# A Strassen-tiled pooling trunk: the second phase's operands stored and loaded, an inner product added in its last block, weight sums and short copies moved

## The chip, the cores and the metric

One core of a Trainium2 chip runs the whole kernel in one launch. The metric is device microseconds of that core, lower is better. The engines are called by the profile's names: PE is the matrix engine (TensorE; PEld its weight loads), DVE VectorE, ACT ScalarE, POOL GpSimd, SP the engine that issues most DMAs.

## The reference, cut to what matters

With DEPTH = 1 only the pooling mixer runs, then a final RMS norm. x is (1, 4096, 1024) in float32.

```python
normed = rms_norm(x, norm_w)
u, gate = split(normed @ pool_in_w, 2)                     # 1024 -> 2 x 1024
pooled = [trailing_mean(u[:, g], 2 << g) for g in 0..3] - u   # windows 2, 4, 8, 16; 256 channels each
mixed = einsum('bsgc,gcd->bsgd', pooled, group_w) + group_b
h = x + (mixed * pool_scale * silu(gate)) @ pool_out_w
out = rms_norm(h, final_norm_w)
```

The group map is folded into the input weights at the start of the kernel, since averaging over time commutes with a map over channels.

## The kernel before, in words

**Three phases.** Steps are written (kind, block, product). In the phases "a" and "b" the rows of x stand in four blocks of 1024; "a" makes the products of the first half of the output channels, "b" those of the second half, from the same normalised x with other weights. Phase "o" is the output projection over eight blocks of 512 rows, followed by the residual, the final norm and the stores. A block's matrix product is one level of Strassen-Winograd: seven products P1 to P7 of half-size operands in the order P1, P2, P7, P6, P5, P4, P3 (`ORDER_IN`). The left operands (weights' sums) are kept in `w`, the right ones (x's sums) are made for each block: "11", "12", "21", "22" are quarters of normalised x; P7's operand replaces "21", P6's (S2) is called "2", P5's (S1) replaces "11", P3's (S4, `form_s4`) replaces "12".

**Splitting.** Each operand is a sum of two reduced-precision float32r parts, so a product is three passes. `split` writes the high part with a ScalarE copy and the low part with a VectorE subtraction; both read the full operand of 128x1024 twice per product (h = 0, 1). A plain product is 48 matmuls of 128x512 (`mm3`, line 807). An inner product (`product_seven`, line 753) applies Strassen once more inside P7: 84 matmuls of 128x256, whose operands `split_seven` makes with sums of half tiles and two further splits, and whose partial sums ScalarE moves between banks. In phase "b" this is done in blocks 1 and 2. Its weight sums take three of the eleven `st` buffers (`kept_in`) and a part of P7's weight buffer, which `load_plain` and `split_plain` fill again with the plain weight for block 3.

**Storage.** Quarters P1, P2, P7 and P4 of normalised x are written to DRAM (`sd`) from GpSimd's queue while phase "a" splits them, and phase "b" reads them back (`load_saved`) on SP's queue; there S2, S1 and S4 are formed on VectorE again. All temporaries come from two pools of equal tiles, eleven `st` and eight `vt`: `take` hands out the tile that was given back longest ago, and a DMA into it waits until its last user is done. Loads are issued three steps ahead (`load_reach`), splits one step ahead (`split_reach`).

**Work beside the products.** Pooling (`pool`) runs on VectorE a step or more after its half block is evicted; a ScalarE copy of 128x32 takes the previous half block's last 16 rows from `tails`, another writes the new ones. `save_t3` forms a weight sum for phase "b" (loads of two stored sums, one subtraction, a store) after step (a, 2, P7). `make_wo` forms the output weights' sums in blocks 1 and 2 of phase "b" and stores them (`wod`); `load_w` reads and splits each into `w[i]` after the last block has used that buffer. The order of instructions on each engine is fixed when the program is built, by the program's order, dependences and hints (`tc.issue_after`: not ahead of that instruction on its engine).

**The end.** From the third output block on, `steady` writes out the order by hand. In the last block the results are normalised in pieces, and the inner part of P2 adds its results with `add_inner` from a spare bank, which TensorE uses again for the next inner product.

Of the kernel before, what the change touches and what calls it, by code (L numbers as in the profile page):

```python
# [10 lines left out]
F32 = mybir.dt.float32  # L11
# [75 lines left out]
def kernel(  # L87
# [115 lines left out]
    def split(dst, src):  # L203
# [17 lines left out]
        for i in range(P1, P7 + 1)  # L221
# [3 lines left out]
            i: [dram.tile([P, 2, H], F32, name=f"sd{b}_{i}_{h}") for h in range(2)]  # L225
            for i in (P1, P2, P7, P4)
        }
# [96 lines left out]

    def save_t3():

        for h in range(2):
# [246 lines left out]
    def load_saved(b, i):  # L574
# [5 lines left out]
        return us  # L580

    def load_in(q, b, i):
        s = xs[b]
        if i == P1:
            s["11"] = load_saved(b, P1) if q else load_x(b, 0, 0)
        elif i == P2:
            s["12"] = load_saved(b, P2) if q else load_x(b, 0, 1)
        elif i == P7:
            s["21"] = load_saved(b, P7) if q else load_x(b, 1, 0)
        elif i == P6:  # L590
            s["22"] = load_saved(b, P4) if q else load_x(b, 1, 1)

    def form_in(q, b, i):

        s = xs[b]
        if i in (P1, P2):
            if q == 0:
                for u in s["11" if i == P1 else "12"]:
                    normalize(b, 0, u)
        elif i == P7:  # L600
            if q == 0:
                for h in range(2):
                    normalize(b, 1, s["21"][h])
                    sub(s["21"][h], s["11"][h], s["21"][h])
        elif i == P6:
            s["2"] = [take(pool=early if (q, b) == (0, 0) else None) for _ in range(2)]
            for h in range(2):
                if q == 0:
                    normalize(b, 1, s["22"][h])
                sub(s["2"][h], s["22"][h], s["21"][h])  # L610
            if not inner_in(q, b, P7):
                for u in s.pop("21"):
                    give(u)
            if q == 0:
                give(rstd.pop(b))
        elif i == P5:
            for h in range(2):
                add(s["11"][h], s["2"][h], s["11"][h])
            if (q, b) != (0, 0) and not inner_in(q, b, P7):
                for u in s.pop("2"):  # L620
                    give(u)

    def inner_in(q, b, i):

        return q == 1 and 0 < b < NB - 1 and i == P7

    def split_in(q, b, i):
        s = xs[b]
        if inner_in(q, b, i):
            return split_seven(s)  # L630
        key = {P1: "11", P2: "12", P6: "2", P7: "21", P5: "11", P4: "22", P3: "12"}[i]
# [62 lines left out]
    def form_seven(stage):  # L694
# [31 lines left out]
        if stage == 3:  # L726
            for u in seven.pop("raw"):
                give(u)

    def load_plain():  # L730
        seven["plain"] = take("p (n k c) -> p n k c", n=2, k=2)
        sync.dma_start(out=seven["plain"][:, 0], in_=t3d[0][:, :, 0:256])

    def split_plain():
        u = seven.pop("plain")
        home = [w[P7][0][:, v, :, 0:256] for v in range(2)]
        copy(home[0], u[:, 0])
        sub(home[1], u[:, 0], home[0].bitcast(F32))
        give(u)

# [319 lines left out]
    def pool(b, q, half, vs, sgs):  # L1060
# [4 lines left out]
        for g in range(2):  # L1065
# [301 lines left out]
    def evict_o(b, i, sets):  # L1367
# [13 lines left out]
        for j in range(2):  # L1381
# [24 lines left out]
            if last:  # L1406
                factors.append(late_factor(half, j, parts))
                if i == P4 and j == 1 or i == P3 and j == 0:
# [65 lines left out]
    def run(n, between=None, behind=None, seeds=4):  # L1474
# [7 lines left out]
        else:  # L1482
            q = 0 if kind == "a" else 1
            if inner_in(q, b, i):
# [6 lines left out]
                product_seven(split_up.pop(n), sets["v"], next_half, next_half)  # L1491
                if b == NB - 2:
                    give_kept(*places_in)
# [8 lines left out]
            if inner_in(q, b, i):  # L1502
                form_s4(b)
                for u in xs[b].pop("2"):
                    give(u)
# [3 lines left out]
    def steady(n):  # L1509
# [87 lines left out]
        elif i == P2:  # L1597
# [4 lines left out]
            ready[P4] = next_op("p (s a b) -> p s a b", **whole)  # L1602
            split(ready[P4], s["22"])
            give(s.pop("22"))
            if final:
                norm_row(b - 1, 0, 1)
            InOrder.on = not final
            product_out(P2, ready.pop(P2), sets, False)
            evict_o(b, P2, sets)
        elif i == P5:  # L1610
            sub(s["12"], s["12"], s["11"])
# [6 lines left out]
        elif i == P4:  # L1618
            if not final:
                ahead["12"] = load_y(c, 0, 1)  # L1620
# [233 lines left out]
    def split_reach(kind, b, i):  # L1854
        if kind == "b" and 0 < b < NB - 1 and i == P6:
            return 0
        return 2 if kind == "o" and (b, i) != (0, P1) else 1

    def row_plan(b):
# [16 lines left out]
        (1, P6): lambda: sum_inner(P7),  # L1876
        (1, P5): lambda: split_weight(P7, P7, P6),
        (1, P4): lambda: (split_weight(P7, P5, P3), keep_temps(P7)),
    }
    forming_seven = (P7, P6, P5, P4)  # L1880

    for n in range(2, len(steps)):
# [72 lines left out]
        if kind in ("a", "b"):  # L1955
# [3 lines left out]
            if kind == "b" and b == NB - 1:  # L1959
                load_w(wod, i)  # L1960
            if kind == "b" and b in (1, 2) and i == P7:
                load_wo(b - 1)
                if b == NB - 2:
                    load_plain()
# [3 lines left out]
            if kind == "b" and b == NB - 2 and i == P4:  # L1968
                with tc.issue_after(latest_copy[0]), tc.issue_after(latest_split[0]):
                    split_plain()  # L1970
            if kind == "b" and b == NB - 1 and i == P3:
# [57 lines left out]
```

## Time and profile before

| what | before |
|---|---|
| time, median of three runs | 907.2 us (907.1 to 908.36) |
| the profiled execution's own time | 907.23 us |
| its span | 905.4 us |
| granted TensorE clock | 0.998 |
| PE / DVE / ACT / POOL busy | 895.8 / 757.0 / 517.5 / 118.5 us |
| DMA | 180.49 MB, mean 199 GB/s |
| first matmul of phase "a", of "o", last matmul's end | 32.6, 613.0, 898.4 us |

The span is what the instructions cover; the execution's own time adds what lies around it. Busy time is summed over instructions; an engine's idle time matters only where TensorE waits for it. Buffer numbers are left out, so `st` stands for eleven buffers. L79 is a helper through which VectorE, ScalarE, GpSimd and SP record everything, so their groups are told apart by tiles.

### The profile page before, as it was taken

The numbers are of one execution on the slowest core, as the hardware profiler recorded it, in microseconds if no ns is written. First come the engines' busy times: TensorE is split into PE (matmuls) and PEld (weight loads), VectorE is DVE, ScalarE is ACT, GpSimd is POOL, SyncE is SP. The second block draws the span as 40 slices with busy tenths as digits, with TensorE's granted clock in tenths as the row PEclk, the third lists the DMA queues.
The fourth block names the chain that finished last, engine by engine and source line by source line (L and its number), as shares of the span: only waits on it lengthen the run. The fifth ranks groups of instructions, "written<-read, shape, count | busy, mean of one in ns | idle before, by whom it ended". The sixth has DMA issues, their size and how long they took to land.

```text
span 905.4 us, 12216 instructions
## 1 busy us (share of the span) xinstructions
PE 895.8 (99%) x4518; PEld 791.1 (87%) x4518; DVE 757.0 (84%) x925; ACT 517.5 (57%) x853; POOL 118.5 (13%) x208
## 2 busy tenths in 40 slices
PE   9999999999999999999999999999999999999996
PEld 7888888888888888889889888888889899999995
DVE  3899995985995999797599499599798878888797
ACT  7869547547445565346545636654657466565464
POOL 0020100100110000000000000001133333343330
PEclk9999999999999999999999999999999999999999
DMA  9987767577675453333554474638483865945953
GB/s 343 401 305 226 273 239 241 187 274 233 235 267 198 164 199 103 99 112 111 202 199 135 179 279 143 197 117 239 143 236 88 212 180 147 233 153 131 259 181 116
DMA packets 71692, 180.49 MB, mean 199 GB/s; under 512 B 6608, under 2 KB 24656, under 8 KB 71632
## 3 DMA queue, kind: packets, MB, share of 16 engines
q1 hardware_dynamic: 54976, 132.50, 42.6%
q0 software_dynamic: 15936, 46.16, 17.6%
q10 hardware_dynamic: 720, 1.06, 0.3%
q8 instruction: 35, 0.57, 0.3%
q14 instruction: 25, 0.20, 0.1%
HBM read 118.86 MB, written 60.83 MB: 198 GB/s over the span
## 4 chain that ended last, share of the span: by engine, by line
PE 87%; DVE 5%; ACT 3%; DMA 2%; issue 2%; POOL 0%; SPq 0%; DVEq 0%; ACTq 0%; POOLq 0%
PE bank L807 78%; PE bank L949 5%; DVE vt L79 2%; PE bank L753 2%; DVE op L79 2%; DMA st<-yd 1%; PE bank L447 1%; DVE st L79 1%; ACT op L79 1%; DMA early<-in_wut 1%; ACT st L79 1%; ACT w L79 0%; ACT vt L79 0%; DMA st<-wod 0%; DVE w L79 0%
## 5 line engine op out<-in xcount | busy, mean ns | idle before, releaser
L807 PE MATMUL bank<-op,w 128*128 128x512 f32 x2592 | 560.9, 379 | 0.1
L807 PEld LDWEIGHTS bank<-op,w 128*128 128x128 f32 x2592 | 489.4, 189 | 70.3 <-ACT vt L79 0.5
L807 PE MATMUL bank<-w,op 128*128 128x512 f32 (+1 forms) x1044 | 230.5, 377 | 0.0
L807 PEld LDWEIGHTS bank<-w,op 128*128 128x128 f32 x1044 | 192.3, 189 | 25.0
L79 DVE TENSOR_TENSOR op<-st,op 128x1024 fp32r<-128x1024 f32 x116 | 141.0, 1222 | 49.7 <-ACT op L79 49.3
L79 ACT ACTIVATE op<-st 128x1024 fp32r<-128x1024 f32 x116 | 121.4, 1051 | 68.7 <-PE bank L807 27.6
L79 ACT ACTIVATE op<-vt 128x1024 fp32r<-128x1024 f32 x67 | 70.4, 1053 | 59.3 <-DVE vt L79 38.7
L79 ACT ACTIVATE vt<-bank 128x512 f32<-128x512 f32 (+1 forms) x124 | 69.6, 580 | 48.0 <-PE bank L807 44.2
L79 DVE TENSOR_TENSOR op<-vt,op 128x1024 fp32r<-128x1024 f32 x67 | 80.9, 1221 | 17.5 <-ACT op L79 17.4
L79 DVE TENSOR_TENSOR st<-st,st 128x1024 f32<-128x1024 f32 (+1 forms) x55 | 63.9, 1181 | 17.6 <-ACT st L79 16.8
L79 POOL DMA_DIRECT2D vt<-in_x x26 | 23.3, 937 | 390.7 <-DVE vt L79 353.8
L79 ACT ACTIVATE bank<-bank 128x512 f32<-128x512 f32 (+1 forms) x78 | 38.7, 498 | 43.5 <-PE bank L807 32.1
L79 DVE TENSOR_TENSOR vt<-bank,vt 128x512 f32<-128x512 f32 (+1 forms) x94 | 54.2, 603 | 7.1 <-PE bank L949 4.6
L79 ACT ACTIVATE st<-bank 128x512 f32<-128x512 f32 (+1 forms) x58 | 33.0, 587 | 31.2 <-PE bank L807 17.4
L79 ACT ACTIVATE st<-st 128x1024 f32<-128x1024 f32 x33 | 34.8, 1056 | 22.6 <-DVE st L79 19.6
L79 DVE TENSOR_TENSOR st<-bank,st 128x512 f32<-128x512 f32 (+1 forms) x68 | 41.2, 625 | 7.4 <-PE bank L807 4.1
L79 DVE TENSOR_TENSOR st<-st,vt 128x1024 f32<-128x1024 f32 (+1 forms) x36 | 41.6, 1175 | 2.2 <-DMA vt<-rd 2.2
L949 PEld LDWEIGHTS bank<-w,op 128*128 128x128 f32 x312 | 40.4, 191 | 1.7
L949 PE MATMUL bank<-w,op 128*128 128x256 f32 x312 | 41.1, 275 | 0.0
L79 DVE TENSOR_TENSOR w<-st,w 128x1024 fp32r<-128x1024 f32 (+1 forms) x27 | 31.6, 1182 | 9.3 <-ACT w L79 9.2
L79 DVE TENSOR_TENSOR_SCAN vt<-vt,window 128x1040 f32<-128x1040 f32 x16 | 38.0, 2381 | 0.3 <-DMA yd<-vt 0.3
L79 DVE TENSOR_TENSOR vt<-vt 128x1024 f32<-128x1024 f32 (+3 forms) x42 | 37.6, 898 | 0.1
(115 smaller groups left out, 720.7 us busy)
## 6 DMA issues: line engine op xcount, KB each, us to landing
st<-in_xt SPq DMA_DIRECT2D x28, 512.0 KB, 6.2
sd<-st POOLq DMA_DIRECT2D x28, 512.0 KB, 4.4
st<-sd SPq DMA_DIRECT2D x26, 512.0 KB, 4.5
st<-in_x SPq DMA_DIRECT2D x21, 512.0 KB, 6.3
yd<-st SPq DMA_DIRECT2D x19, 512.0 KB, 2.9
vt<-yd SPq DMA_DIRECT2D x17, 512.0 KB, 10.4
out<-vt POOLq DMA_DIRECT2D x17, 512.0 KB, 3.3
st<-wod SPq DMA_DIRECT2D x16, 512.0 KB, 4.3
```

The source lines that it names most:

```text
L79: r = f(*args, **kwargs)
L447: latest[0] = nc.tensor.matmul(ps, a[:, kk, 2 * j + t, :], maps, start=t + m == 0, stop=t == 1 and m == len(pairs) - 1,).ins
L753: latest[0] = nc.tensor.matmul(cell(n, c).rearrange("p (a s) -> p a s", s=2), x1, x2, start=i == P1 and k + m == 0, stop=k == 1 and m == 2 ...
L807: latest[0] = nc.tensor.matmul(ps, a, b, start=start and n == 0, stop=stop and n == 2, skip_group_check=True).ins
L949: latest[0] = nc.tensor.matmul(ps, x1, x2, start=start and k + n == 0, stop=k == 1 and n == 2, skip_group_check=True,).ins
```

## The change

It has these parts. (1) Phase "a" stores the operands of all seven products, except block 0's S2, and phase "b" loads them instead of forming them; block 0's S2 is still formed there from "22" and "21". An operand's tiles are given back after its split. (2) The inner P7 is used in block 3 as well, so the plain weight is no longer restored and the three `st` buffers are held until block 3's P7. (3) In block 3 of phase "b" the output weights are loaded and split in other groups: P1's after P7, P2's and P7's after P6, P6's and P5's after P5; their splits come behind the step's evictions. (4) The weight sum T3 is formed in two halves, after (a, 1, P3) and (a, 2, P3). (5) In phase "b" the short copy from `tails` runs on GpSimd. (6) In the output phase, the first inner addition of the last block precedes P2's evictions, P4's split comes after them, one row normalisation moves to P4's stage, and two of the inner weight splits move one step later.

```diff
-            for i in (P1, P2, P7, P4)
+            for i in range(P1, P7 + 1)
+            if (b, i) != (0, P6)
...
 def load_w(src, i):
-            split(w[i][h], u)
+            with tc.issue_after(evicted[0]):
+                split(w[i][h], u)
...
+    operand = {P1: "11", P2: "12", P7: "21", P6: "2", P5: "11", P4: "22", P3: "12"}
     def load_in(q, b, i):
         s = xs[b]
-        if i == P1:
-            s["11"] = load_saved(b, P1) if q else load_x(b, 0, 0)
...
-        elif i == P6:
-            s["22"] = load_saved(b, P4) if q else load_x(b, 1, 1)
+        if q and (b or i not in (P6, P4)):
+            s[operand[i]] = load_saved(b, i)
+        elif q:
+            if i == P6:
+                s["22"] = load_saved(b, P4)
...
     def inner_in(q, b, i):
-        return q == 1 and 0 < b < NB - 1 and i == P7
+        return q == 1 and b > 0 and i == P7
...
 def split_in(q, b, i):
-        if i == P6 and (q or b):
+        if i == P6 and q == 0 and b:
             form_s4(b)
-        if i not in (P1, P2, P7, P6):
+        if q and (b or i != P7) or i not in (P1, P2, P7, P6):
             for u in s.pop(key):
                 give(u)
...
 def pool(b, q, half, vs, sgs):
+            elif q:
+                gpsimd.tensor_copy(out=v[:, :, 0:HIST], in_=tails[:, g])
             else:
                 copy(v[:, :, 0:HIST], tails[:, g])
...
 def evict_o(b, i, sets):
         if inner and i == P2:
             inner["rows"] = [hs[b][0, j][:, 0] for j in range(2)]
+            if final:
+                add_inner(0, (0, 0))
...
-        if inner and i == P2:
+        if inner and i == P2 and not final:
             add_inner(0, (0, 0))
...
 def form(n):
-        if kind in ("a", "b"):
-            form_in(kind == "b", b, i)
+        if kind == "a":
+            form_in(b, i)
+        elif (kind, b, i) == ("b", 0, P6):
+            s["2"] = [take() for _ in range(2)]
+            for h in range(2):
+                sub(s["2"][h], s["22"][h], s["21"][h])
...
 def steady(n), i == P2:
-            split(ready[P4], s["22"])
-            give(s.pop("22"))
-            if final:
-                norm_row(b - 1, 0, 1)
+            if not final:
+                split(ready[P4], s["22"])
+                give(s.pop("22"))
             InOrder.on = not final
             product_out(P2, ready.pop(P2), sets, False)
             evict_o(b, P2, sets)
+            if final:
+                split(ready[P4], s["22"])
+                give(s.pop("22"))
...
 i == P4:
+            if final:
+                norm_row(b - 1, 0, 1)
...
 forming = {
-        (1, P5): lambda: split_weight(P7, P7, P6),
-        (1, P4): lambda: (split_weight(P7, P5, P3), keep_temps(P7)),
+        (1, P4): lambda: (split_weight(P7, P7, P6, P5, P3), keep_temps(P7)),
...
 main loop
-        if kind == "a" and b == 2 and i == P7:
-            save_t3()
+        if kind == "a" and b in (1, 2) and i == P3:
+            save_t3(b - 1)
...
-                load_w(wod, i)
+                for p in {P1: (), P2: (), P7: (P1,), P6: (P2, P7), P5: (P6, P5)}.get(i, (i,)):
+                    load_w(wod, p)
```

More of the change, by code (lines that the diff above doesn't have):

```diff
@@ L323, in load_wb, with save_t3 @@
                     sync.dma_start(out=p[name], in_=place)
-    def save_t3():
-        for h in range(2):
+    def save_t3(*hs):
+        for h in hs:
             us = []
@@ L580, in load_saved, with form_in @@
         return us
+    operand = {P1: "11", P2: "12", P7: "21", P6: "2", P5: "11", P4: "22", P3: "12"}
     def load_in(q, b, i):
         s = xs[b]
-        if i == P1:
-            s["11"] = load_saved(b, P1) if q else load_x(b, 0, 0)
[L586 to L589, printed above, removed]
-        elif i == P6:
-            s["22"] = load_saved(b, P4) if q else load_x(b, 1, 1)
-    def form_in(q, b, i):
+        if q and (b or i not in (P6, P4)):
[3 more added lines that the diff above has]
+                s["22"] = load_saved(b, P4)
+        elif i in (P1, P2, P7, P6):
+            key, *place = {
+                P1: ("11", 0, 0), P2: ("12", 0, 1), P7: ("21", 1, 0), P6: ("22", 1, 1)
+            }[i]
+            s[key] = load_x(b, *place)
+    def form_in(b, i):
         s = xs[b]
         if i in (P1, P2):
-            if q == 0:
-                for u in s["11" if i == P1 else "12"]:
-                    normalize(b, 0, u)
+            for u in s["11" if i == P1 else "12"]:
+                normalize(b, 0, u)
         elif i == P7:
[L601 to L604, printed above, removed]
+            for h in range(2):
+                normalize(b, 1, s["21"][h])
+                sub(s["21"][h], s["11"][h], s["21"][h])
         elif i == P6:
-            s["2"] = [take(pool=early if (q, b) == (0, 0) else None) for _ in range(2)]
+            s["2"] = [take(pool=early if b == 0 else None) for _ in range(2)]
             for h in range(2):
-                if q == 0:
-                    normalize(b, 1, s["22"][h])
+                normalize(b, 1, s["22"][h])
                 sub(s["2"][h], s["22"][h], s["21"][h])
[L611 to L615, printed above, removed]
+            for u in s.pop("21"):
+                give(u)
+            give(rstd.pop(b))
         elif i == P5:
@@ L618, in form_in @@
                 add(s["11"][h], s["2"][h], s["11"][h])
-            if (q, b) != (0, 0) and not inner_in(q, b, P7):
+            if b:
                 for u in s.pop("2"):
@@ L630, in split_in @@
             return split_seven(s)
-        key = {P1: "11", P2: "12", P6: "2", P7: "21", P5: "11", P4: "22", P3: "12"}[i]
+        key = operand[i]
         later = q == 0 and b == 0 and i in (P1, P2)
@@ L728, in form_seven @@
                 give(u)
[L730 to L739, printed above, removed]
     def product_seven(t, v, middle, end):
@@ L1455, in form @@
         kind, b, i = step(n)
-        if kind in ("a", "b"):
-            form_in(kind == "b", b, i)
+        if kind == "a":
+            form_in(b, i)
+        elif (kind, b, i) == ("b", 0, P6):
+            s = xs[b]
+            s["2"] = [take() for _ in range(2)]
+            for h in range(2):
+                sub(s["2"][h], s["22"][h], s["21"][h])
+            for u in s.pop("21"):
+                give(u)
     def split_step(n):
@@ L1491, in run @@
                 product_seven(split_up.pop(n), sets["v"], next_half, next_half)
-                if b == NB - 2:
+                if b == NB - 1:
                     give_kept(*places_in)
@@ L1502, in run @@
             if inner_in(q, b, i):
-                form_s4(b)
                 for u in xs[b].pop("2"):
@@ L1618, in steady @@
         elif i == P4:
-            if not final:
+            if final:
+                norm_row(b - 1, 0, 1)
+            else:
                 ahead["12"] = load_y(c, 0, 1)
@@ L1854, in split_reach @@
     def split_reach(kind, b, i):
-        if kind == "b" and 0 < b < NB - 1 and i == P6:
+        if kind == "b" and b > 0 and i == P6:
             return 0
@@ L1959 @@
             if kind == "b" and b == NB - 1:
-                load_w(wod, i)
+                for p in {P1: (), P2: (), P7: (P1,), P6: (P2, P7), P5: (P6, P5)}.get(i, (i,)):
+                    load_w(wod, p)
             if kind == "b" and b in (1, 2) and i == P7:
                 load_wo(b - 1)
-                if b == NB - 2:
-                    load_plain()
             if kind == "b" and b in (1, 2) and i == P6:
@@ L1967 @@
                     make_wo(b - 1)
-            if kind == "b" and b == NB - 2 and i == P4:
-                with tc.issue_after(latest_copy[0]), tc.issue_after(latest_split[0]):
-                    split_plain()
             if kind == "b" and b == NB - 1 and i == P3:
```

## The prediction

> **What bounds the kernel now.** I read the page's head first, then TensorE's timeline, then the chain, then the busy time by stage.
>
> ```profile
> span 905.4 us, 12216 instructions
> PE 895.8 (99%) x4518; PEld 791.1 (87%) x4518; DVE 757.0 (84%) x925; ACT 517.5 (57%) x853; POOL 118.5 (13%) x208
> ```
>
> TensorE is busy 895.8 of 905.4 us. The timeline says where it is not (last bracket: idle before, and who ended it):
>
> ```profile
> 498.68 114.46 PE L807 MATMUL bank<-op,w 128*128 128x512 f32 x528
> ...
> 671.19 0.94 PE L949 MATMUL bank<-inner,op 128*128 128x256 f32 x6 [0.31 <-DVE vt L79]
> ...
> 885.05 0.94 PE L949 MATMUL bank<-inner,op 128*128 128x256 f32 x6 [0.61 <-DVE vt L79]
> ...
> 887.78 10.61 PE L807 MATMUL bank<-w,op 128*128 128x512 f32 x60
> ```
>
> After the start TensorE waits twice, 0.31 and 0.61 us, and both times for VectorE in the output phase. In the second phase (steps "b", 323 to 613 us) it does not wait at all: the first row is eleven products in one piece, up to the phase's end. The last row ends at 898.39, so 7.0 us of the span are what follows the last matmul. The chain gives the price of a product:
>
> ```profile
> 46.72 370.76 PE bank L807 x1716
> 417.48 9.60 PE bank L753 x84
> 427.08 62.16 PE bank L807 x288
> 489.24 9.60 PE bank L753 x84
> ```
>
> Line 807 is a plain product: 370.76/1716 = 0.2161 us a matmul (62.16/288 = 0.2158 in the second piece), and 48 of them make 10.37 us. Line 753 is the inner P7 of blocks 1 and 2: 84 matmuls of half the width, 9.60 us both times.
>
> ```profile
> 105.30:177.90 72.60, 72.60 (x338) 63.56 (x337) 62.45 (x75) 40.24 (x67) 6.69 (x13) 1.00 0.67 226
> ...
> 323.20:395.90 72.70, 72.70 (x338) 63.67 (x337) 64.10 (x77) 36.60 (x52) 0.00 (x0) 1.00 0.41 137
> ...
> 539.60:613.00 73.40, 73.34 (x341) 63.89 (x340) 63.44 (x61) 40.87 (x58) 0.00 (x0) 1.00 0.46 154
> ```
>
> Columns: stretch, length, then busy us of PE, weight loads, DVE, ACT and POOL, granted clock, DMA share, GB/s. A block of seven products takes 72.6 us and TensorE fills it; VectorE fills 62 to 64 us of it, ScalarE 37 to 41, GpSimd nothing in the second phase, and the clock is full. So whatever only relieves VectorE or ScalarE is worth nothing here unless it ends one of the two waits; what counts is TensorE's own work, and whether a new wait arises.
>
> **The change part by part.**
>
> *Inner P7 in the last block.* Block 3's P7 becomes the 84 small matmuls: 10.37 - 9.60 = 0.77 us off TensorE. That is the one certain term. In a sentence of its own: the Trainium skill (TensorE: Matmul & The Clock Gate, "Step-by-step: what each phase is for") gives a gap of N/2.4 ns plus 2.5 ns, and by it this would be an estimated 10.36 - 9.17 = 1.18 us. The trace agrees for N = 512 (216 ns) but not for this product, which takes 114 ns a matmul; I keep 0.77.
>
> What feeds it is VectorE and ScalarE work:
>
> ```profile
> L79 DVE TENSOR_TENSOR op<-st,op 128x1024 fp32r<-128x1024 f32 x116 | 141.0, 1222 | 49.7 <-ACT op L79 49.3
> L79 ACT ACTIVATE op<-st 128x1024 fp32r<-128x1024 f32 x116 | 121.4, 1051 | 68.7 <-PE bank L807 27.6
> ```
>
> ```profile
> 496.83 0.70 DVE L79 TENSOR_TENSOR bank<-bank,vt 128x512 f32<-128x512 f32 x1 [0.88 <-PE bank L753]
> ```
>
> Two more splits than the plain product (2 x 1.22 on VectorE, 2 x 1.05 on ScalarE), and six half-width additions at 0.70 (four sums, two on the banks): 2.4 + 4.2 = 6.6 us of VectorE. The loaded operands take six formations (two each for S2, S1 and S4; VectorE takes 1.22 for any addition or subtraction of this size) from the same block, 7.3 us. Net -0.7, so a block that VectorE fills to 63 of 73 us stays where it was, and 0.77 is not given back there.
>
> *Operands stored and loaded.* Blocks 1 to 3 lose six formations each and block 0 loses four: 22 x 1.22 = 27 us of VectorE, all in a stage where TensorE never waits for it: worth 0. What comes in is 22 stores in the first phase and 22 loads in the second, 512 KB each.
>
> ```profile
> sd<-st POOLq DMA_DIRECT2D x28, 512.0 KB, 4.4
> st<-sd SPq DMA_DIRECT2D x26, 512.0 KB, 4.5
> ```
>
> ```profile
> 216.84 0.54 POOL L79 DMA_DIRECT2D rd<-rs  x1 [20.27 <-DVE rs L79]
> ```
>
> Per block that is six transfers of 0.52 MB in 72.6 us, 43 GB/s more. From the window rows the first phase goes from 226 to 269 GB/s, a share of about 0.67 x 269/226 = 0.80; the second from 137 to 180, about 0.54. Neither is full. A DMA issue costs GpSimd's queue 0.54 us, six of them 3.2 us a block, in a queue that idled 20.27 us ahead of the row-statistics store (rd), which is the thing that stands behind the new stores. That gap, 196.6 to 216.8, runs from P2 to P6 of block 2 (which starts at 177.9, 10.37 us a product), where S2, S1 and S4 are formed and the new stores become ready, so I price the delay of rd at 0; its bound is the 3.2 us, against an x operand loaded three steps, 31 us, ahead. A tile whose store is pending is given back after its split; the store lands 4.4 us after issue, and needs the formed tile alone, not its split, which comes a product or so later: 0.
>
> *SP's queue.* The loads pass SP's in-order queue, past the stores of pooling (yd) and of the output weights (wod). Of the four rows below the third is a wait of ScalarE for a saved operand:
>
> ```profile
> 439.32 7.52 SPq L79 DMA_DIRECT2D wod<-st  x5
> ...
> 450.29 5.50 SPq L79 DMA_DIRECT2D st<-sd  x5
> ```
>
> ```profile
> 456.98 1.06 ACT L79 ACTIVATE op<-st 128x1024 fp32r<-128x1024 f32 x1 [0.93 <-DMA st<-sd]
> ...
> 559.47 1.06 ACT L79 ACTIVATE w<-st 128x1024 fp32r<-128x1024 f32 x1 [5.88 <-DMA st<-wod]
> ```
>
> That wait was for block 2, due at 468: hidden. The new loads for P5, P4 and P3 are asked for at the start of steps P2, P7 and P6, ahead of the weight stores that step P6 ends with, and each operand's tiles are given back after one split instead of being held for the block, so tiles come free sooner. I take 0; the upper bound is the first rival.
>
> *Output weights loaded in groups in the last block*, their splits put behind the eviction. Before, a late wod tile held ScalarE 5.88 us (row above) and TensorE ran on. Work is the same 14 splits, moved two steps later into steps P6 and P5, four halves each (4 x 1.22 = 4.9 of VectorE's 10.4 us). Also 0, with the second rival as its bound. The restored plain quarter of P7's weight goes (one copy, one subtraction of half width, off the path), T3's two halves are formed at other steps with the same instructions: 0.
>
> *Pooling's short copies on GpSimd.*
>
> ```profile
> L79 ACT ACTIVATE vt<-tails 128x32 f32<-128x32 f32 x28 | 6.3, 228 | 45.7 <-DVE vt L79 35.1 <-DMA yd<-vt 4.5 <-DVE inner L79 3.6
> ```
>
> ```profile
> 864.82 1.18 POOL L79 TENSOR_TENSOR otmp<-otmp,ors 128x2 f32<-128x2 f32 x1
> ...
> 866.36 0.19 POOL L79 TENSOR_TENSOR ors<-ors,otmp 128x2 f32<-128x2 f32 x1
> ```
>
> Fourteen of the 28 copies leave ScalarE (3.2 us, and part of 45.7 us in which they held its queue for VectorE). No GpSimd copy is in the trace; by its nearest rows one costs 0.19 us, or 1.18 when VectorE runs a two-input addition beside it, so 3 to 17 us in all. The copy waits for the tile that ScalarE evicts; behind it in GpSimd's queue is nothing in this phase, on VectorE the window sum of the same half block waits for it, and ScalarE's next copy into the tails. VectorE has 9 us a block to spare and just got 7: 0. The Trainium skill (SBUF — State Buffer, "Who interferes with whom") says a VectorE instruction with two SBUF inputs and a GpSimd one that reads SBUF exclude each other for the whole instruction. The 1.18 against 0.19 agrees; it speaks against this move, but the cover holds by the rows above.
>
> *Final block.* The first inner addition now precedes P2's evictions, and P4's split and one row normalisation come after.
>
> ```profile
> 881.04 1.22 DVE L79 TENSOR_TENSOR op<-vt,op 128x1024 fp32r<-128x1024 f32 x1
> 882.18 1.28 DVE L79 SCALAR_TENSOR_TENSOR vt<-vt,ors,st 128x1024 f32<-128x1024 f32 x1
> 883.37 1.62 DVE L79 TENSOR_TENSOR vt<-bank,vt 128x512 f32<-128x512 f32 x3
> ...
> 898.71 0.41 DVE L79 TENSOR_TENSOR vt<-bank,vt 128x256 f32<-128x256 f32 x1
> ```
>
> The three evictions at 883.37 are what TensorE's 0.61 us wait at 885.05 is for; without the 2.5 us in front of them it goes. But VectorE has no gap from 882 to the end, and its last addition starts 0.3 us after the last matmul, so the same instructions in another order end the kernel hardly sooner. Between 0 and 0.61 I take the middle, 0.30: what stands ahead is late next.
>
> **Sum**, against the profiled execution (span 905.4, time 907.23, so 1.8 us lie around the span; the median of the runs is 907.2, the same): 907.2 - 0.77 - 0.30 = 906.1, a tenth of a per cent.
>
> **The rivals.** What a measurement of this kernel can tell from no change is about 0.2%, 1.8 us: 905.4 to 909.0 counts as the same.
>
> *Slower: SP's queue.* Place: blocks 1 and 2, whose step P6 puts the weight stores on SP. If tiles are not free in time, P3's loads slip behind those stores into the burst of 450.29. P3 starts at 427.08 + 3 x 10.37 = 458.2; the first half needs copy and subtraction, 1.06 + 1.22, so it decides at a landing of 455.9. As early as the 456.98 row, TensorE waits 1.1 us; as the last of the five loads (issued at 455.8, landing 4.5 later), 4.4. Twice: 2.2 to 8.8; at 4 us, 910.1. For it: SP did stand 7.52 us in those stores, and a load was late. Against it: the program order.
>
> *Slower: the weight groups.* In block 3, if ScalarE's queue takes a weight split ahead of an operand's copy and waits for the load. 5.88 us passed unseen; four tiles that arrive one after another could hold it up to about twice that, and the excess, some 5 us, would show: 911. Against it: these splits now stand behind the eviction, and the loads start a step ahead of it.
>
> *Nothing gained.* The inner product waits for a split or a move, as it has never done in blocks 1 and 2, and the end eats the rest: 907.2.
>
> *All of it.* Both waits go in full and the slow places in the phases' rhythm too: 371 us at 0.2161 against 0.2158 are 0.5. 0.77 + 0.61 + 0.31 + 0.5 = 2.2: 905.0.
>
> **How the numbers follow.** Forecast 906.1 (from 905.5 to 906.9): 0.47. Nothing gained: 0.08. All of it: 0.16. SP's queue: 0.15. Weight groups and any other new wait of that size: 0.14. So faster 0.16, same 0.55, slower 0.29. The range begins at 904.8, just under the best case, and reaches 911.5, past the middle of both slow ones.
>
> **What would show it.** Right: a third line-753 group of 84 matmuls, 9.6 us, in block 3; no idle before a PE row between 47 and 610 us; no 0.61 near 884; VectorE some 27 us less busy, GpSimd with 14 short copies of 0.2 to 1.2 us; 22 more sd stores and 22 more loads. Wrong: an idle time of over 1 us before a line-807 row, with its releaser: ScalarE or VectorE's op at P3 of blocks 1 and 2 with ScalarE waiting for sd means the first rival, op or w in block 3 with ScalarE waiting for wod the second. A span under 903.5 would mean the end of the kernel is worth more than I gave it.

## The result: slower by 0.4%, and the profile after

| | before | after |
|---|---|---|
| time, median of six runs | 907.39 us (907.1 to 908.36) | 911.38 us (909.14 to 912.72) |
| ratio | | 1.0041, interval 1.0026 to 1.0055 |
| the profiled execution: time, span | 907.23, 905.4 us | 911.84, 910.1 us |
| last matmul's end | 898.4 us | 902.6 us |

The heads of the page of after, against those of before:

```profile
span 910.1 us, 12426 instructions
...
PE 896.9 (99%) x4554; PEld 792.7 (87%) x4554; DVE 737.6 (81%) x910; ACT 518.5 (57%) x848; POOL 144.7 (16%) x244
...
DMA packets 77756, 203.30 MB, mean 223 GB/s; under 512 B 7296, under 2 KB 25088, under 8 KB 77696
...
PE 67%; DVE 15%; issue 4%; ACT 3%; DMA 2%; POOL 0%; DVEq 0%; ACTq 0%; POOLq 0%
```

VectorE lost 19 us of work and the kernel became slower. What moved is the DMA (180.49 to 203.30 MB) and the chain that ends last: 67% of it is TensorE, 87% before, and VectorE's share went from 5% to 15%. The third inner product is there and costs what it should. It is this row of that chain:

```profile
566.88 9.60 PE bank L743 x84
```

TensorE's timeline shows where it was not busy (start, length, what, count, and in the bracket the idle time before and who ended it):

```profile
202.52 219.46 PE L797 MATMUL bank<-op,w 128*128 128x512 f32 x1008 [2.59 <-ACT vt L79]
...
560.14 6.74 PE L797 MATMUL bank<-op,w 128*128 128x512 f32 x30 [1.10 <-ACT bank L79]
...
676.26 0.94 PE L939 MATMUL bank<-inner,op 128*128 128x256 f32 x6 [0.60 <-DVE vt L79]
...
891.98 10.61 PE L797 MATMUL bank<-w,op 128*128 128x512 f32 x60
```

Two idle times are new: 2.59 us in the *first* phase (block 2's P7), where the prediction named no rival, and 1.10 us in block 3's P2. The first costs more than it shows. Busy times by stretch around it (columns as in the prediction):

```profile
199.00:202.00 3.00, 0.93 (x5) 0.47 (x3) 3.00 (x4) 0.25 (x2) 1.06 (x2) 1.00 0.68 208
202.50:205.60 3.10, 3.08 (x7) 2.52 (x8) 2.58 (x3) 3.10 (x6) 1.53 (x4) 0.50 0.95 329
206.00:209.00 3.00, 3.00 (x15) 2.63 (x14) 2.02 (x2) 1.89 (x3) 0.02 (x1) 1.00 0.89 350
```

For 3.1 us after the idle TensorE's granted clock is 0.50 and seven matmuls run where fifteen fit: they take 0.43 us instead of 0.216, another 1.5 us. So this one place costs some 4 us: start to start 2.97 instead of 0.22, and the seven. With the wait at 560 and the inner product's gain the output projection begins 4.8 us late (617.76 for 612.98 us). Who was late at 202? ScalarE's rows, after first, then before:

```profile
201.75 0.23 ACT L79 ACTIVATE vt<-tails 128x32 f32<-128x32 f32 x1 [5.50 <-DVE vt L79]
201.89 2.04 ACT L79 ACTIVATE vt<-bank 128x512 f32<-128x512 f32 x4
```

```profile
196.83 0.23 ACT L79 ACTIVATE vt<-tails 128x32 f32<-128x32 f32 x1 [5.50 <-DVE vt L79]
196.97 1.07 ACT L79 ACTIVATE vt<-bank 128x512 f32<-128x512 f32 x2
```

The four evictions that free P7's banks stand behind a short copy, which waits for VectorE as it did before, and VectorE is 4.9 us late. Its own rows of after say why:

```profile
95.33 1.23 DVE L79 TENSOR_TENSOR st<-st,vt 128x1024 f32<-128x1024 f32 x1 [3.79 <-DMA vt<-rd]
...
163.48 1.23 DVE L79 TENSOR_TENSOR st<-st,st 128x1024 f32<-128x1024 f32 x1 [3.26 <-DMA st<-wvd]
```

The first is block 1's row statistics (in before at 93.83 with an idle of 2.16). They come 1.5 us late, but from 140 to 160 us VectorE is busy for only 11.2 us of 20 and can make that good. The second is T3's first half at its new place: its loads are late, the instruction behind the next split stands at 165.76 instead of 161.91, and an addition of pooling that had come before it (1.1 us) now comes after it. Together these are the 4.9 us. From 180 to 200 us VectorE is busy for 19.9 of 20, so the delay is still there when P7 needs the banks.

The sum, in the span: +2.75 and +1.5 at 202, +1.05 at 560 (1.27 start to start above a matmul's length; 0.22 in block 3 of before), +0.3 at 676, -0.77 for the inner product, -0.6 for the wait at 885 that went, +0.5 behind the last matmul: 4.7, from 905.4 to 910.1.

### The profile page after: what moved, and what is told of

Its sections match the earlier page's. It is cut to its first block, busy times and chain, and to the rows that moved or that the text cites. A ratio compares the mean times of both kernels' runs of the same rounds, so it can differ in the third digit from the quotient of the medians.

```text
span 910.1 us, 12426 instructions
## 1 busy us (share of the span) xinstructions
PE 896.9 (99%) x4554; PEld 792.7 (87%) x4554; DVE 737.6 (81%) x910; ACT 518.5 (57%) x848; POOL 144.7 (16%) x244
## 2 busy tenths in 40 slices
DMA packets 77756, 203.30 MB, mean 223 GB/s; under 512 B 7296, under 2 KB 25088, under 8 KB 77696
## 4 chain that ended last, share of the span: by engine, by line
PE 67%; DVE 15%; issue 4%; ACT 3%; DMA 2%; POOL 0%; DVEq 0%; ACTq 0%; POOLq 0%
PE bank L797 58%; DVE vt L79 6%; PE bank L939 6%; DVE st L79 5%; DVE op L79 3%; PE bank L743 3%; ACT st L79 1%; ACT vt L79 1%; ACT op L79 1%; DMA vt<-rd 1%; DMA st<-wvd 1%; DMA wod<-vt 0%; DVE columns L79 0%; ACT L79 0%; POOL vt L79 0%
## 5 line engine op out<-in xcount | busy, mean ns | idle before, releaser
L797 PE MATMUL bank<-op,w 128*128 128x512 f32 x2544 | 552.8, 380 | 3.7 <-ACT vt L79 2.6
L797 PEld LDWEIGHTS bank<-op,w 128*128 128x128 f32 x2544 | 481.4, 189 | 73.5 <-ACT vt L79 3.0
L79 DVE TENSOR_TENSOR op<-st,op 128x1024 fp32r<-128x1024 f32 x118 | 143.9, 1223 | 71.5 <-ACT op L79 71.1
L79 ACT ACTIVATE op<-st 128x1024 fp32r<-128x1024 f32 x118 | 123.8, 1052 | 93.6 <-PE bank L797 29.6
L79 ACT ACTIVATE vt<-bank 128x512 f32<-128x512 f32 (+1 forms) x120 | 66.4, 576 | 46.8 <-PE bank L797 40.0
L79 DVE TENSOR_TENSOR st<-st,st 128x1024 f32<-128x1024 f32 (+1 forms) x46 | 50.4, 1105 | 20.9 <-ACT st L79 16.8
L79 POOL COPY vt<-tails 128x32 f32<-128x32 f32 x14 | 14.7, 1058 | 302.5 <-ACT tails L79 138.5
L79 ACT ACTIVATE st<-bank 128x512 f32<-128x512 f32 (+1 forms) x64 | 36.7, 589 | 39.3 <-PE bank L797 28.8
L79 POOL DMA_DIRECT2D sd<-st x44 | 23.5, 534 | 129.1 <-DVE st L79 79.5
L79 DVE TENSOR_TENSOR st<-st,vt 128x1024 f32<-128x1024 f32 (+1 forms) x32 | 36.8, 1169 | 4.2 <-DMA vt<-rd 3.8
```

The costliest lines, as they stand in the source:

```text
L79: r = f(*args, **kwargs)
L797: latest[0] = nc.tensor.matmul(ps, a, b, start=start and n == 0, stop=stop and n == 2, skip_group_check=True).ins
```

## The experiments

All ratios are to the kernel before, run on the same chip.

### T3 or the stores?

Two things are new ahead of 202 us: T3's halves, with loads in the middle of block 1, and 22 stores from GpSimd's queue.

**t3_back**: after, with T3 formed at its old place.

```diff
-        if kind == "a" and b in (1, 2) and i == P3:
-            save_t3(b - 1)
+        if kind == "a" and b == 2 and i == P7:
+            save_t3(0, 1)
```

> The changed kernel with T3 formed in one go after (a, 2, P7), as before. Theory A (the moved T3 half: VectorE loses 3.3 us of waiting for its load and 1.2 us of work in the stretch before block 2, ScalarE's eviction of P2 comes 4.9 us late, TensorE idles 2.6 us and then runs seven matmuls at half speed): no idle near 200 us, about 4.4 us less than the changed kernel, 907.0; the 1.1 us idle near 556 stays. Rival B (the 22 new stores slow the first phase and T3 only met them): VectorE still 1.5 us or more late, an idle of 1 us or more stays near 200, 908.5 or more.

Measured: 912.32 us (911.28 to 914.1), 1.006 [1.0048, 1.0072]. The idle at 202 went, and one of 3.33 us came at 223, where T3's loads now were. So T3's place picks the spot and not the loss.

**t3_alone**: before, with T3 in halves at its new places.

> The kernel before with nothing changed but T3 formed in halves after (a, 1, P3) and (a, 2, P3). Theory A: VectorE is 3 to 4.5 us late before block 2, which is 1 to 2.3 us more than there is to spare, so an idle of 1 to 2.3 us at 199 to 203 and the half-speed matmuls (1.5 us) after it: 909.5 to 911. Rival B: without the new stores the half fits: 907.4.

Measured: 908.08 us (906.25 to 911.55), 1.0011 [1.0001, 1.0021], and no idle of TensorE in the first phase of the profiled run (907.34 us). Its first two loads landed 5.1 us after their issue (median) and VectorE waited 1.05 us for them; in after it was 7.3 and 3.26 us, with a DMA share of 0.98 and 0.89 from 140 to 150 and 150 to 160 us instead of 0.70 and 0.74. Moving T3 is nearly free without the stores.

**stores_alone**: before, with the 22 stores, which nothing reads.

```diff
-            for i in (P1, P2, P7, P4)
+            for i in range(P1, P7 + 1)
+            if (b, i) != (0, P6)
```

> The kernel before with the 22 new stores added and nothing that reads them: the operands are still formed in the second phase. Theory S (the stores of S2, S1 and S4 stand in one burst, 3 MB in some 12 us, and whatever is loaded behind them comes late): DMA share of 200 to 210 us near 1.0 instead of 0.52, VectorE waits 3 to 4 us for T3's loads or the row statistics, TensorE idles 2 us or more between 195 and 225, then runs some matmuls at half speed: 910 to 912. Rival (the stores are hidden, and another part or the loads make it late): no idle there, 907.2 to 907.6.

Measured: 912.77 us (912.4 to 913.64), 1.0061 [1.0049, 1.0073]: the stores alone lose as much as the whole change. (Of its span, 0.7 us is another place: TensorE waits 1.34 us at 890, where it waited 0.61 before.) Its timeline, on TensorE, VectorE and ScalarE:

```profile
223.14 198.70 PE L808 MATMUL bank<-op,w 128*128 128x512 f32 x912 [3.22 <-ACT st L79]
```

```profile
210.86 1.23 DVE L79 TENSOR_TENSOR st<-st,st 128x1024 f32<-128x1024 f32 x1 [3.34 <-DMA st<-wvd]
...
221.18 1.23 DVE L79 TENSOR_TENSOR st<-st,st 128x1024 f32<-128x1024 f32 x1 [4.09 <-DMA st<-wvd]
```

```profile
222.49 2.06 ACT L79 ACTIVATE st<-bank 128x512 f32<-128x512 f32 x4 [6.65 <-DVE st L79]
```

A load is late, VectorE waits for it, ScalarE's eviction waits for VectorE, TensorE for the bank. The first loads were asked for no later than before (their rows on SP's queue: before, then stores_alone):

```profile
201.49 7.01 SPq L79 DMA_DIRECT2D st<-wvd  x3
213.67 0.33 SPq L79 DMA_DIRECT2D st<-wvd  x1
```

```profile
200.90 7.02 SPq L79 DMA_DIRECT2D st<-wvd  x3
216.02 0.33 SPq L79 DMA_DIRECT2D st<-wvd  x1
```

They took longer. T3's first pair from issue to landing (the last column, median us), before, then stores_alone:

```profile
st<-wvd SPq DMA_DIRECT2D x2, 512.0 KB, 3.8
```

```profile
st<-wvd SPq DMA_DIRECT2D x2, 512.0 KB, 8.3
```

The last load stands behind the store of T3's first half (t3d), for which SP's queue waited, so it was asked for 2.35 us later. Next the last two columns, the DMA engines' share and GB/s, for ten microseconds each; before, then stores_alone:

```profile
200.00:210.00 10.00, 10.00 (x49) 8.74 (x48) 6.67 (x7) 7.15 (x11) 0.00 (x0) 1.00 0.52 174
210.00:220.00 10.00, 10.00 (x48) 8.77 (x47) 4.99 (x10) 6.49 (x10) 0.54 (x1) 1.00 0.93 319
```

```profile
200.00:210.00 10.00, 10.00 (x48) 8.77 (x47) 4.67 (x5) 6.95 (x11) 1.60 (x3) 1.00 0.98 374
210.00:220.00 10.00, 9.92 (x46) 8.34 (x45) 5.73 (x10) 5.81 (x9) 0.54 (x1) 1.00 0.99 356
```

GpSimd's queue issues eight stores of operands between 195.0 and 207.9 us, where before it issued two: S1, S2 and S4 of a block are formed close together, so their stores come as a burst, where T3's weights and the next block's x are fetched. The share from 200 to 210 us, 0.52, becomes 0.98. That the stores make the loads late is shown; that they do it by filling the DMA engines is read from these shares.

**late_t3**: can T3 be moved out of the crowd? After, with the halves at (a, 2, P3) and (a, 3, P1) and seed_first's edit (below).

```diff
-        if kind == "a" and b in (1, 2) and i == P3:
-            save_t3(b - 1)
+        if (kind, b, i) in (("a", 2, P3), ("a", 3, P1)):
+            save_t3(b - 2)
```

> The kernel after with block 3's inner operands split behind the evictions (as in seed_first) and T3's halves moved to (a, 2, P3) and (a, 3, P1), behind the crowded stretch of the DMA queues (160 to 220 us). Theory S (the stores crowd the DMA engines and whoever loads there is late): the row statistics are still 1.5 us late in block 1, but no st<-wvd load holds VectorE ahead of 200 us, so TensorE's idle at 199 (1.6 us in seed_first) falls under 0.5 and none comes at 220. Theory V (VectorE runs without a gap from 584 to 672 us, so whatever TensorE gains before that it waits for at 672): the wait at 672 grows by what was gained, from 1.7 to about 3.3 us, and the span stays at 906.8 (time 908.5 to 910). Against V: the span falls by the 1.6 us, to 905.2, time 907.

Measured: 911.26 us (910.86 to 913.14), 1.0048 [1.0036, 1.006]. The idle at 199 went, as expected, and I had not expected the next one, 2.07 us at 275. This time no T3 load is in it; ScalarE's rows of late_t3 show a pooling store that had not left its tile:

```profile
274.78 0.23 ACT L79 ACTIVATE vt<-tails 128x32 f32<-128x32 f32 x1 [5.84 <-DMA yd<-vt]
```

The share from 270 to 280 us is 0.98, 0.50 before, and that store took 7.4 us from its issue to its landing. But seed_first has the same share of 0.98 there and no idle: with T3 elsewhere, its copy had come at 261.44. So there is a crowd in each of blocks 1 to 3, and it costs time where a transfer that an engine is about to need falls into it.

### The wait at 560 us, and the short copies

ScalarE moves P1's last bank at 559.51, behind a copy for the inner product's first operand, which had waited 5.37 us for VectorE. **seed_first** puts block 3's inner operands behind the step's evictions.

```diff
-            with tc.issue_after(evicted[0]) if i == P6 else nullcontext():
+            behind = i == P6 or (kind, b, i) == ("b", NB - 1, P7)
+            with tc.issue_after(evicted[0]) if behind else nullcontext():
```

> The changed kernel with the split of block 3's inner operands issued behind the evictions of P1 on ScalarE; no instruction more or fewer. Theory: the last of the four copies of P1's result waited 5.4 us behind a split that waited for VectorE's sums, and TensorE 1.3 us for that copy. The idle at 560 goes and 1.3 us with it: 910.1. Rival (VectorE's backlog itself is late for the inner product): the idle moves to the inner product's start at 566, time as the changed kernel, 911.4.

Measured: 910.17 us (908.23 to 911.56), 1.003 [1.0018, 1.0042]; the idle at 560 is gone, so the cause of that wait is shown. But TensorE waits 1.67 us at 673 instead of 0.60. The profiled run (908.6 us) also idles only 1.61 us at 201, with full clock behind it, so the difference to after is not this edit's alone. **both** joins it with t3_back:

> Both of the edits before. If the two causes are all that was lost, TensorE has no idle between 47 and 617 us and the time is that of the changed kernel less 4.4 and 1.3: 905.7 to 906.2, 0.1 to 0.2% below the kernel before. If the new stores or loads cost something of their own: 907 or more.

Measured: 912.6 us (911.44 to 915.41), 1.0063 [1.0051, 1.0075]; in the profiled run, the slowest of the five, TensorE waits 3.95 us at 224 and 2.37 at 678.

**act_copies**: after, with the short copies on ScalarE again.

> The changed kernel with pooling's short copies on ScalarE again. If the move is worth nothing, as I forecast, the same time as the changed kernel, 911.4, within 0.5. Rival: a GpSimd copy holds VectorE up (1.06 us a copy in the changed kernel, where ScalarE took 0.23), and without it the second phase has 1 us less of idle: 910.3.

Measured: 912.27 us (910.0 to 914.63), 1.0055 [1.004, 1.007]: no gain against after's 1.0041. In the profiled run the wait at 560 is 0.36 us instead of 1.10, as the rival says, but the one at 676 is 1.34 instead of 0.60, which takes it back.

### Without storing the operands

**formed**: both, but S2, S1 and S4 formed in the second phase as in before; no new store or load.

> The changed kernel with T3 formed as before, with block 3's inner split behind the evictions, and with the operands formed in the second phase as before: no new store and no new load is left; inner P7 in block 3, the weight groups, the GpSimd copies and the final block are as in the changed kernel. Theory S: no idle before 600 us, 0.8 us gained in block 3. Theory V (VectorE is full from 590 to 672 us, since the groups put two more weight splits there, so what TensorE gains in block 3 it waits for in the second output block): an idle of 1 to 2 us near 670, 906.5 to 907.2. Without V: 905.9 to 906.2.

Measured: 908.2 us (907.91 to 910.54), 1.0017 [1.0008, 1.0026]. No idle in the first phase: that loss was the stores'. It is still not faster than before. TensorE's waits in formed (total us, times, longest):

```profile
PE bank L938 <- DVE vt L79: 1.4, 1, 1.4
PE bank L742 <- DVE op L79: 0.9, 2, 0.7
```

**formed_early_w**: formed, with the weight groups `{P7: (), P6: (P7, P6)}`, each other product's weight loaded at its own step.

> The kernel named formed with the output weights loaded and split as early as each buffer allows: P1 after P1, P2 after P2, P7 and P6 after P6, the rest after their own step. Theory V: two weights' splits return to the stretch of 545 to 570 us, the idle near 670 falls to 0.5 us or less, 0.5 to 1.5 us less than formed: 905.5 to 906.2. Rival (the splits fill the place that the inner product's operands need): a new idle in block 3, no better than formed.

Measured: 920.49 us (919.3 to 924.07), 1.0151 [1.0134, 1.0169]. In block 3's inner product TensorE waits 2.00, 0.88 and 5.37 us, while ScalarE waits 1.97, 3.32 and 1.14 us for st<-wod with a weight copy. This is the prediction's second rival; part (3) of the change is what keeps it away.

### The wait at 672 us

My reading was that VectorE, without a gap from 584 us on, was simply full. **late_t3_groups** and **formed_groups** fill an idle stretch of VectorE at 579 us with weight splits, in late_t3 and in formed: groups `{P1: (), P2: (), P7: (P1, P2), P6: (P7, P6)}`.

> As late_t3, and the output weights of block 3 in groups one step earlier: P1's and P2's after P7, P7's and P6's after P6, P5's, P4's and P3's each after their own step. Theory V: VectorE idled 4.4 us at 579 us for the grouped weights and then ran full; two to four splits of 1.22 us fall into that gap, so the run of VectorE ends 2.4 to 4.9 us earlier, TensorE's wait at 672 goes under 0.5 us, and the span is about 903.6 to 904.5, time 905.4 to 906.5: faster than both kernels. Rival (weight groups): ScalarE's copies wait for the wod loads in front of an operand's copy, TensorE waits 1 us or more before a plain product between 575 and 612 us, and the time is 908 or more.

> formed (operands formed in the second phase as before, inner P7 in block 3, T3 and its loads where they were, block 3's inner operands behind the evictions) with the weight groups of late_t3_groups. Theory V: the wait at 672 (1.4 us, 1.81 start to start) goes under 0.5, span 905.0 to 905.4, time 906.6 to 907.2. Rival: the groups themselves hold TensorE in block 3 or V is wrong, time 908 or more as formed.

Measured: 913.89 us (911.19 to 916.71), 1.0071 [1.0056, 1.0086], and 913.81 us (911.32 to 915.14), 1.0068 [1.0054, 1.0082]. The waits at 672 grew to 2.8 us in both, so this theory fell, though in block 3 itself TensorE waited 0.25 us at most. What grew with them is a wait that I had passed over. VectorE's rows at 645 us, in formed and in formed_groups:

```profile
645.66 0.69 DVE L79 TENSOR_TENSOR st<-st,st 128x512 f32<-128x512 f32 x1 [1.16 <-DMA st<-wod]
```

```profile
647.59 0.69 DVE L79 TENSOR_TENSOR st<-st,st 128x512 f32<-128x512 f32 x1 [3.19 <-DMA st<-wod]
```

It is the load of the output phase's first inner weight sum (`load_inner(P2)`). On SP's queue it stands behind pooling's stores; in formed:

```profile
634.22 2.90 SPq L79 DMA_DIRECT2D yd<-vt  x2
637.95 0.32 SPq L79 DMA_DIRECT2D st<-wod  x1
```

In before it was issued at 633.84 and VectorE did not wait; in formed_groups it was issued at 643.11, behind a load into a `vt` tile for which SP's queue had waited 6.5 us, until the tile's pooling store had landed. **seed_early** asks for it one step earlier in seed_first:

```diff
-        (0, P4): lambda: load_inner(P2),
+        (0, P5): lambda: load_inner(P2),
```

> seed_first (the kernel after with block 3's inner operands behind the evictions) with load_inner(P2) at (o, 0, P5). Theory L: VectorE's 1.38 us wait for st<-wod at 645 goes, TensorE's wait at 673 falls from 1.7 to 0.3 us, span 905.4, time 908.7. Theory V: no change, 910.2.

VectorE's wait went, and TensorE's at 674 fell to 0.3 us, as expected: the late load is the cause of this wait. The time did not follow: 910.52 us (908.64 to 912.37), 1.0033 [1.0021, 1.0046]. In its profiled run the idle at 202 is 2.8 us with half clock behind it, against 1.61 us without in seed_first's, so here the two profiles differ by the crowd, which varies from run to run.

### A version that beats both

**formed_act**: formed with the short copies on ScalarE.

> formed with the short copies back on ScalarE. Theory G (in formed a GpSimd copy that waits for its tile's pooling store stood, by way of VectorE's queue, ahead of the front sums of block 2's inner product): VectorE's 1.89 us wait for POOL at 485.8 and TensorE's waits of 0.66 and 0.25 us at 491.8 to 493.9 go, the output phase begins 0.9 us sooner; the time falls by 0.9 to 907.3 unless it is waited for again at 672. Rival (the copies cost nothing, the order of VectorE does): the waits at 491 stay and the time stays at 908.2.

Measured: 907.34 us (905.77 to 910.09), 1.0000 [0.9991, 1.0009]; the waits at 492 are gone, and the profiled run, one of the slower (909.29 us), waits 1.97 us at 671. In formed GpSimd's copy had waited for a pooling store, and VectorE for the copy, ahead of the inner product's front sums:

```profile
485.76 0.17 DVE L79 TENSOR_REDUCE window<-vt 128x1 f32<-128x16 f32 x1 [1.89 <-POOL vt L79]
```

**formed_act_early** adds seed_early's edit, **formed_act_early2** the same at `(0, P6)`.

> formed_act with the loads of the output phase's first inner weight sums (load_inner(P2)) asked for at (o, 0, P5) instead of (o, 0, P4), 5.2 us earlier in the program's order. Theory L (that load, behind the pooling stores on SP, lands late; VectorE waits for it at 645 us, and TensorE for VectorE at 672): VectorE's wait for st<-wod (1.16 us in formed) goes and TensorE's wait at 672 falls from 1.4 us to 0.3, as before; span about 904.4 to 904.8, time 906.2 to 906.6, just ahead of before. Theory V (VectorE is full): the wait at 672 stays over 1.2 us and the time is within 0.4 of formed_act.

> As formed_act_early, the loads asked for at (o, 0, P6), 10.4 us earlier. Theory L: the same as formed_act_early or better (906.2 to 906.6). If the tiles are not free that early, the loads hold SP's queue and the loads of y behind them come late: a wait of TensorE before 672 us and 908 or more.

Measured: 906.27 us (905.05 to 907.36), 0.9984 [0.9975, 0.9993], and 906.29 us (905.13 to 908.15), 0.9988 [0.998, 0.9997]. Both are faster than before, by 0.1 to 0.2%, and than after. formed_act_early keeps parts (2), (3) and (6) of the change, drops (1), (4) and (5), and adds two edits of order. Its head and VectorE's row at 643 us, now without a wait:

```profile
span 903.9 us, 12301 instructions
```

```profile
643.11 0.69 DVE L79 TENSOR_TENSOR st<-st,st 128x512 f32<-128x512 f32 x1
```

TensorE's wait behind it did not fall to the expected 0.3 us: it is 0.74 us in this profile and 1.10 in formed_act_early2's, against 1.97 in formed_act. VectorE's wait for the load had been 1.04 us in formed_act, and about that much went; the rest has another cause, which no run here shows.

```profile
670.16 0.94 PE L938 MATMUL bank<-inner,op 128*128 128x256 f32 x6 [0.74 <-DVE vt L79]
```

### The end

**end_alone**: before, with part (6) alone.

> The kernel before with only the last block's reordering (first inner addition ahead of P2's evictions, P4's split behind them, one row normalisation at P4's stage, two inner weight splits one step later). The prediction's term: TensorE's 0.61 us idle at 885 goes, the end gains 0 to 0.61 us, I took 0.30: span 904.8 to 905.4, time 906.7 to 907.3. Other theory: the last VectorE addition sets the end, span 905.4 as before. A loss (over 907.8) would mean the later inner weight splits are late.

Measured: 907.57 us (906.63 to 908.52), 1.0001 [0.9992, 1.001]. The 0.61 us wait is gone and the last matmul ends at 898.14 instead of 898.40, but 7.9 us follow it instead of 7.0: VectorE's last normalisation starts at 901.26 (900.73 before).

## Why the prediction was wrong

- **The step that failed: the operands' stores, priced at 0.** I compared the DMA's share averaged over a 72 us block, 0.67 rising to 0.80, and wrote "Neither is full". As means these are about right (0.80 in block 1 of after), but they say nothing of shorter stretches. In after the share rose from 0.72 and 0.75 to 0.98 and 0.89 between 140 and 160 us, where T3's first loads fall; in stores_alone it rose from 0.52 and 0.93 to 0.98 and 0.99 between 200 and 220 us. Loads in these stretches came late, and the stores alone cost 0.6%. The store's landing, 4.4 us in the prediction, was 6.2 us. The forecast was 0.1% faster, and the kernel became 0.4% slower. That 911.4 us still lies inside my range is luck: its upper end came from rivals in the second phase, and most of the loss came in the first.
- **rd's bound.** I bounded the delay of the row statistics by GpSimd's issue time, 3.2 us. They were 1.5 us late in block 1, but not by the issue: GpSimd issued their store at 81.02, at 81.16 before. The store took 6.4 us to land instead of 5.1, so their load was issued at 88.01 instead of 86.86, and it took 7.3 us instead of 7.0.
- **T3 at 0.** "At other steps with the same instructions" left out that each half has two loads, whose time depends on where they fall. Alone it is nearly right (1.0011); beside the stores it is wrong, because T3's loads are the ones that came late.
- **Inner P7, -0.77.** The size is right: 9.60 us. (By the formula quoted beside it, the estimate is 1.19 us and not 1.18; nothing rests on it.) "Not given back" was wrong. I summed VectorE's work over the block and did not look at ScalarE's order, where the operand's copy stood ahead of an eviction: 1.3 us.
- **The rivals.** SP's queue in blocks 1 and 2 did not happen: no idle there. The weight groups as built did not hold TensorE; formed_early_w shows that the mechanism is real. Neither is what happened.
- **VectorE's relief, worth 0.** VectorE lost 19 us of work and nothing was gained, but no run has the relief without the stores; what speaks for 0 is that TensorE did not wait in the second phase of before. My sign "some 27 us less busy" forgot the 6.6 us that I had put down for the inner product.
- **GpSimd's copies at 0.** In after this is right for the time (act_copies), though one wait moved. The copies took 14.7 us, 1058 ns each in the mean, near my upper bound of 1.18, and up to 2.15 us. In formed, where VectorE still forms the operands, the same copies cost TensorE 0.9 us.
- **The end, -0.30.** The argument, that the same instructions in another order end hardly sooner, held; the value did not: 0.0, within 0.1% either way.

What stays open is the run-to-run spread of after (909.14 to 912.72 us), since only one of its runs was profiled. The half clock is not all of it: 3.4 us at 0.50 lower the mean granted clock by 0.0019, and the two runs with a mean of 0.999, which leaves no room for that, took 910.56 and 910.93 us. Also open is what the 22 new loads of the second phase cost by themselves: no run adds them alone.

## What to carry to other kernels

Price added traffic in the ten microseconds where it falls, not over a stage: means of 0.71 before and 0.80 after hid stretches at 0.93 and 0.98, and a new burst can make late any load or store that shares its window. When a stall moves with each edit (202, 223, 275 us), stop moving its victims and take away the one thing that all versions share. An in-order engine or queue carries a small wait far: a late load, an engine that waits for it and an eviction behind that reached TensorE 12 us later at 223, 27 at 672 and 39 at 202.

## What the runs showed of the hardware

- In these traces every idle time of TensorE of 2.07 us or more in the middle of the kernel was followed by a granted clock of 0.50 for 3.41 us (6.83 us once in the run both, 10.24 in formed_early_w): six to eleven plain matmuls at 0.43 us instead of 0.216, a few matmuls later where narrow ones came first. Up to 1.86 us left none; about 2.0 went both ways (1.97 us in formed_act, eight; 2.01 us at 683 in formed_early_w, none). At that point an idle time's price jumps by about 1.5 us. The Trainium skill (TensorE: Matmul & The Clock Gate, "Part 1: The HAM clock gate") gives 426.7 ns for a cold matmul of N = 512, which these agree with, and has the clock fall after an idle window of about 3.4 us; here 2.07 was enough.
- Over ten microseconds the DMA engines moved 374 GB/s in the crowd of stores_alone, 379 in that of late_t3 (270 to 280 us) and 381 in that of t3_back (200 to 210 us). The most was at the start of the kernel, 403 GB/s from 30 to 40 us in before. The Trainium skill (DMA: Bandwidth & Descriptors, "Specifications") gives 435 GB/s as the fabric's ceiling and about 358 as the HBM's limit for one core; the trace is above the second.
